# The last output pair's products in another order, and one product of the first set in column halves

## The chip, the cores and the metric

The kernel runs on one core of a Trainium2 chip. The metric is the device time of one execution in microseconds (us), median of several runs. "The span" is the time from the first to the last instruction of the one execution that the profiler recorded; it is about 1.8 us shorter than the device time of the same execution.

## The reference, cut to what matters

```python
def reference(x, w1, w2):            # x 16x256x512, w1 512x4096, w2 2048x512, all float32
    h = x @ w1
    gate, value = np.split(h, 2, axis=-1)
    h = np.maximum(gate, 0) * value
    return (h @ w2).astype(np.float32)
```

## The kernel before

Both matrix products are done block by block with seven half-size products (P1 to P7) instead of eight, in float16. The 4,096 rows of x are worked off in four sets of 1,024. In each set 16 blocks fill `g` (the hidden values), and four pairs of row tiles then turn `g` into output. A checker on the side looks whether the values suit float16; if not, a slow general way runs behind a branch at the end. For these inputs the branch is taken over the general way.

```python
# the whole program: the fast way, then a branch over the general way
with ExitStack() as fast:
    unfit = fast_way(fast, tc, x2, w1, w2, out2, flag)
with tc.If(unfit > 0, label="general"):
    with ExitStack() as general:
        general_way(general, tc, x2, w1, w2, out2)
```

```python
class Block:                                   # one product of the first stage: two 512-column matmuls
    def mm(self, name, ps, fresh):
        wn, xn = WX[name]
        for b in range(2):
            nc.tensor.matmul(ps, wop[wn][:, b, self.jb * P:(self.jb + 1) * P], self.xo[xn][:, b, :],
                             start=fresh and b == 0, stop=b == 1, skip_group_check=True)
    ...
class Pair:                                    # second stage: each product is eight 256-column matmuls
    ...
    def send(self, h, c):
        nc.sync.dma_start(out=out_v[self.s, h, self.t, :, c], in_=self.o[:, h, c])
    ...
    def P2(self):                              # ScalarE evicts X into the left half of the first output
        self.o = tmp.tile([P, 2, DO], F32, name="o", tag="tmp")
        nc.scalar.activation(self.o[:, 0, :DO // 2], self.X, COPY, scale=1 / GS)
        if self.end:
            self.send(0, slice(0, DO // 2))
    ...
    def P7(self):                              # VectorE evicts Y into the right half of the second output
        nc.vector.scalar_tensor_tensor(out=self.o[:, 1, DO // 2:], in0=self.Y, scalar=1 / GS, in1=self.pu[:, 0],
                                       op0=MULT, op1=ADD)
        if self.end:
            self.send(1, slice(DO // 2, DO))

    def P4(self):                              # P4 is added to the same Y; ScalarE evicts it: the last of all
        nc.scalar.activation(self.o[:, 1, :DO // 2], self.Y, COPY, scale=1 / GS)
        self.send(1, slice(0, DO // 2 if self.end else DO))
    ...
ORDER = ("P1 0, P1 1, P2 0, P2 1, P1 2, P5 0, P2 2, P6 0, P3 0, P7 0, P5 1, P6 1, P3 1, P7 1, P4 0, P5 2, P4 1, "
         "P6 2, P3 2, P7 2, P1 3, P4 2, P5 3, P2 3, P6 3, P3 3, P7 3, P4 3")
LAST_ORDER = ORDER.replace("P5 3, P2 3, P6 3, P3 3, P7 3", "P2 3, P6 3, P5 3, P7 3, P3 3")
```

In the last set the order thus ends: P7 2, P1 3, P4 2, P2 3, P6 3, P5 3, **P7 3, P3 3, P4 3** (product, then pair). P4 3 adds to the PSUM bank that P7 3's eviction reads, so its first matmul waits for that eviction.

## Time and profile before

| | before |
|---|---|
| time, median of 3 runs | 308.57 us (308.36 to 308.63) |
| span of the profiled run | 307.2 us |
| TensorE busy | 301.6 us, 98% |
| end of the last matmul | 303.03 us |
| last DMA packet | 305.84 us |

The profile's page of the kernel before: TensorE's busy time, the instruction-fetch queue (packets, MB, share of 16 DMA engines) and the chain of waits that ended last.

```profile
PE 301.6 (98%) x1905; PEld 184.2 (60%) x1905; DVE 236.0 (77%) x388; ACT 176.3 (57%) x348; POOL 151.2 (49%) x189
...
q8 instruction: 16, 0.26, 0.4%
...
PE 96%; DMA 2%; SPq 1%; issue 0%; ACT 0%
```

The windows of the last set and of the tail, kernel before. Columns: stretch, its length, busy us (and instructions) of each engine, granted clock, DMA share, GB/s.

```profile
232.50:303.05 70.55, 70.53 (x438) 42.42 (x436) 56.23 (x93) 32.61 (x65) 31.45 (x48) 1.00 0.14 45
303.05:307.20 4.15, 0.00 (x0) 0.00 (x0) 0.00 (x0) 0.38 (x1) 0.00 (x0) 0.94 0.23 72
```

TensorE has no hole in the last set, and it stands still for 4.15 us behind it. Those four microseconds are the tail: an eviction of 0.38 us, the last send, and the closing barrier.

The timeline of the sending queue in the tail, kernel before. Columns: start, duration of the issue, what.

```profile
299.11 1.04 SPq L370 DMA_DIRECT2D out_dram<-o  x1
...
301.84 0.33 SPq L370 DMA_DIRECT2D out_dram<-o  x1
302.65 0.33 SPq L370 DMA_DIRECT2D out_dram<-o  x1
303.48 1.34 SPq L370 DMA_DIRECT2D out_dram<-o  x1
```

These are the sends of P2, P7, P3 and P4 of the last pair. Two of the four issues are stretched from 0.33 us to over 1 us. An instruction packet of 16 KB began at 298.45 us and another at 303.15 us, shortly before each (read from the trace's packet records).

VectorE's timeline and the branch instructions, kernel before: P7's eviction, then P3's; and the closing branch in TensorE's queue (duration in ns, start).

```profile
301.39 0.42 DVE L399 SCALAR_TENSOR_TENSOR o<-Y,pu 128x256 f32<-128x256 f32 x1 [3.56 <-PE Y L362]
302.20 0.42 DVE L394 SCALAR_TENSOR_TENSOR o<-W,pu 128x256 f32<-128x256 f32 x1 [0.38 <-PE W L362]
```

```profile
L42 PEldq COMPARE_BRANCH  x1: 496/496/496, 301.9 to 301.9; - x1
```

TensorE's sequencer executed the branch at 301.89 us.

The windows of half a microsecond in the tail, kernel before (last two columns: DMA share, GB/s).

```profile
303.50:304.00 0.50, 0.00 (x0) 0.00 (x0) 0.00 (x0) 0.00 (x0) 0.00 (x0) 1.00 0.69 234
304.00:304.50 0.50, 0.00 (x0) 0.00 (x0) 0.00 (x0) 0.00 (x0) 0.00 (x0) 1.00 0.08 12
304.50:305.00 0.50, 0.00 (x0) 0.00 (x0) 0.00 (x0) 0.00 (x0) 0.00 (x0) 1.00 0.09 16
305.00:305.50 0.50, 0.00 (x0) 0.00 (x0) 0.00 (x0) 0.00 (x0) 0.00 (x0) 1.00 0.31 109
305.50:306.00 0.50, 0.00 (x0) 0.00 (x0) 0.00 (x0) 0.00 (x0) 0.00 (x0) 1.00 0.48 158
```

Most of P3's send moves before 304 us. Then only a trickle moves for 1.3 us, and the last send follows. In the packet records the trickle is 16 of the 128 packets of P3's send; of the 16 four-byte packets that follow a send's data, two came late as well (304.73 and 305.14 us, the other 14 by 303.98). That is two DMA engines' worth if a send is spread evenly over the 16 (8 packets and one four-byte packet each; an estimate from these counts, since no view names a packet's engine). Two instruction packets, of 16 KB and of 8 KB, lay before it.

### The profile page before, as it was taken

To read this page: it belongs to the slowest core of one execution; us is meant where nothing else is said; L and a number is where in the kernel's file an instruction comes from. 1 tells how busy PE (TensorE), PEld (TensorE's weight loads), DVE (VectorE), ACT (ScalarE), POOL (GpSimd) and SP (SyncE) were. 2 spreads that over 40 slices of the span, in tenths; PEclk is the share of its full clock that TensorE was granted. 3 is DMA by queue.
4 is the path that set the end of the run, shared out by engine and by line. 5 is a ranking of instruction groups with operands and counts; after the bars stand their busy time and mean duration, and the time that the engine had idled before them with its cause. 6 is when DMAs were issued, how large, how long until landed. Compare 5 with 4: busy or idle time off the path is not lost.

```text
span 307.2 us, 5283 instructions
## 1 busy us (share of the span) xinstructions
PE 301.6 (98%) x1905; PEld 184.2 (60%) x1905; DVE 236.0 (77%) x388; ACT 176.3 (57%) x348; POOL 151.2 (49%) x189
## 2 busy tenths in 40 slices
PE   8999999999999999999999999999999999999994
PEld 7744444588844444478864444458884444447883
DVE  2579888899778888887538888888536888888851
ACT  2488896455865555537855555546866555553231
POOL 2389999800068999300029889700007988700000
PEclk9999999999999999999999999999999999999999
DMA  6985779965775270001354910000325110001132
GB/s 204 358 259 179 239 171 176 229 123 80 260 209 88 69 137 3 0 0 55 136 182 108 207 34 2 0 2 9 130 101 174 35 34 0 3 1 34 54 106 87
DMA packets 35836, 32.87 MB, mean 107 GB/s; under 512 B 14432, under 2 KB 31328, under 8 KB 35680
## 3 DMA queue, kind: packets, MB, share of 16 engines
q1 hardware_dynamic: 33536, 26.22, 28.3%
q0 software_dynamic: 2272, 6.29, 11.4%
q8 instruction: 16, 0.26, 0.4%
q14 instruction: 12, 0.10, 0.1%
HBM read 27.26 MB, written 12.58 MB: 130 GB/s over the span
## 4 chain that ended last, share of the span: by engine, by line
PE 96%; DMA 2%; SPq 1%; issue 0%; ACT 0%
PE Y L250 26%; PE X L250 17%; PE W L250 17%; PE Y L362 14%; PE W L362 9%; PE X L362 9%; DMA x_A<-in_x_dram 2%; PE X L325 1%; PE W L325 1%; PE Y L325 1%; PE Y L498 0%; PE X L498 0%; SPq L217 0%; SPq L488 0%; ACT o L405 0%
## 5 line engine op out<-in xcount | busy, mean ns | idle before, releaser
L250 PEld LDWEIGHTS <-w_T 128*128 128x128 f16 x496 | 48.3, 98 | 57.3 <-POOL w_T L232 1.1
L179 POOL TENSOR_TENSOR fold<-xh 128x1024 f32<-128x1024 f16 x16 | 30.3, 1894 | 94.6 <-DMA xh<-x 93.7
L250 PE MATMUL X<-x_A,w_B 128*128 128x512 f16 x248 | 73.8, 379 | 0.0
L250 PE MATMUL Y<-x_S,w_T 128*128 128x512 f16 x220 | 65.5, 379 | 0.0
L250 PEld LDWEIGHTS <-w_B 128*128 128x128 f16 x372 | 36.3, 98 | 42.1
L277 DVE SCALAR_TENSOR_TENSOR cc<-W,pu 128x512 f32<-128x512 f32 x62 | 42.9, 691 | 21.1 <-ACT pu L271 21.1
L257 ACT COPY Y<-X 128x512 f32<-128x512 f32 x62 | 35.4, 571 | 38.2 <-PE X L250 37.9
L271 ACT ACTIVATE pu<-Y 128x512 f32<-128x512 f32 x62 | 37.1, 598 | 33.9 <-PE Y L250 33.0
L182 POOL TENSOR_TENSOR fold<-fold 128x512 f32<-128x512 f32 (+2 forms) x96 | 51.8, 539 | 7.5
L362 PEld LDWEIGHTS <-w_stage 128*128 128x128 f16 x512 | 50.0, 98 | 5.9
L287 DVE SCALAR_TENSOR_TENSOR cc<-Y,pu 128x512 f32<-128x512 f32 x62 | 42.9, 691 | 6.7
L282 DVE SCALAR_TENSOR_TENSOR g<-X,cc 128x512 f16<-128x512 f32 x62 | 42.8, 691 | 2.3
L299 DVE SCALAR_TENSOR_TENSOR g<-Y,cc 128x512 f16<-128x512 f32 x62 | 42.2, 681 | 1.8 <-PE Y L250 1.8
L362 PEld LDWEIGHTS <-g 128*128 128x128 f16 x384 | 37.5, 98 | 8.2
L264 ACT ACTIVATE pu<-W 128x512 f32<-128x512 f32 x62 | 37.2, 600 | 0.8 <-PE W L250 0.6
L250 PE MATMUL W<-x_S,w_B 128*128 128x512 f16 x124 | 36.9, 379 | 0.0
L250 PE MATMUL W<-x_S,w_T 128*128 128x512 f16 x124 | 36.9, 379 | 0.0
L250 PE MATMUL Y<-x_A,w_T 128*128 128x512 f16 x124 | 36.9, 379 | 0.0
L362 PE MATMUL X<-w,g 128*128 128x256 f16 x256 | 31.9, 273 | 0.0
L394 DVE SCALAR_TENSOR_TENSOR o<-W,pu 128x256 f32<-128x256 f32 x16 | 6.8, 423 | 19.4 <-PE W L362 19.4
L169 DVE TENSOR_TENSOR w_stage<-g 128x1024 f16<-128x1024 f16 x32 | 21.4, 684 | 0.2
L232 POOL TENSOR_TENSOR w_T<-w_stage 128x512 f16<-128x512 f32 (+1 forms) x16 | 18.7, 1173 | 2.5 <-DMA w_stage<-in_w_dram 2.5
(100 smaller groups left out, 307.5 us busy)
## 6 DMA issues: line engine op xcount, KB each, us to landing
w_stage<-in_w_dram SPq DMA_DIRECT2D x14, 512.0 KB, 6.0
out_dram<-o SPq DMA_DIRECT2D x26, 256.0 KB, 2.1
x<-in_x_dram POOLq DMA_DIRECT2D x4, 1024.0 KB, 9.1
xh<-x SPq DMA_DIRECT2D x16, 256.0 KB, 3.0
w<-in_w_dram POOLq DMA_DIRECT2D x2, 1024.0 KB, 10.2
out_dram<-o SPq DMA_DIRECT2D x12, 128.0 KB, 1.7
w_stage<-in_w_dram SPq DMA_DIRECT2D x4, 256.0 KB, 5.4
x_S<-in_x_dram SPq DMA_DIRECT2D x4, 256.0 KB, 6.5
```

What stands on the lines that cost most here:

```text
L169: eng.tensor_tensor(o[n], o[i0], o[i1], op=op)
L179: nc.gpsimd.tensor_tensor(fold, t, t, op=MULT)
L182: nc.gpsimd.tensor_tensor(fold[:, :, :m], fold[:, :, :m], fold[:, :, m:2 * m], op=ADD)
L250: nc.tensor.matmul(ps, wop[wn][:, b, self.jb * P:(self.jb + 1) * P], self.xo[xn][:, b, :], start=fresh and b == 0, stop=b == 1, skip_group ...
L257: nc.scalar.copy(out=self.Y, in_=self.X)
L264: nc.scalar.activation(self.p5, self.W, COPY, scale=GS)
L271: nc.scalar.activation(self.u2, self.Y, COPY, scale=GS)
L277: nc.vector.scalar_tensor_tensor(out=self.c12, in0=self.W, scalar=GS, in1=self.u2, op0=MULT, op1=ADD)
L282: nc.vector.scalar_tensor_tensor(out=self.g[:, self.jb, :TH], in0=self.X, scalar=0.0, in1=self.c12, op0=MAX, op1=MULT)
L287: nc.vector.scalar_tensor_tensor(out=self.c22, in0=self.Y, scalar=GS, in1=self.p5, op0=MULT, op1=ADD)
L299: nc.vector.scalar_tensor_tensor(out=self.g[:, self.jb, TH:], in0=self.Y, scalar=0.0, in1=self.c22, op0=MAX, op1=MULT)
L362: nc.tensor.matmul(ps, self.op[an][:, i], vop[wn][:, i], start=name in ("P1", "P5") and i == 0, stop=i == NJ // 2 - 1, skip_group_check=True)
```

## The change

The intent, as far as the diff shows it: P7 of the last pair, with its eviction and its send, comes four products ahead of the end in place of two, so that less is left for the last microseconds. P1 of that pair moves ahead of P7 of the pair in front to make room. In the first set each P5 is done as four matmuls of 256 columns in place of two of 512.

```diff
+        def __init__(self, xo, g, jb, in_halves=()):
...
-            for b in range(2):
-                nc.tensor.matmul(ps, wop[wn][:, b, ...], self.xo[xn][:, b, :],
-                                 start=fresh and b == 0, stop=b == 1, skip_group_check=True)
+            for c in (half, other) if name in self.in_halves else ((0, TH),):
+                for b in range(2):
+                    nc.tensor.matmul(ps[:, slice(*c)], wop[wn][:, b, ...],
+                                     self.xo[xn][:, b, slice(*c)], start=fresh and b == c[0] == 0, stop=b == 1,
+                                     skip_group_check=True)
... (the output tile is now made by whichever of P2 and P7 comes first)
-    LAST_ORDER = ORDER.replace("P5 3, P2 3, P6 3, P3 3, P7 3", "P2 3, P6 3, P5 3, P7 3, P3 3")
+    LAST_ORDER = ORDER.replace("P7 2, P1 3, P4 2, P5 3, P2 3, P6 3, P3 3, P7 3",
+                               "P1 3, P7 2, P6 3, P5 3, P7 3, P4 2, P2 3, P3 3")
...
-        blocks = {jb: Block(xo, g, jb) for jb in range(first, NJ)}
+        blocks = {jb: Block(xo, g, jb, () if s else ("P5",)) for jb in range(first, NJ)}
...
+            if s == NS - 1 and t == 3:
+                sums = (sum_of(pairs[3].op, n) for n in ("S1", "S2", "S3", "S4"))
```

The halves add 56 instructions to TensorE's program (14 blocks, two more matmuls and two more weight loads each).

More of the change, by code (lines that the diff above doesn't have):

```diff
@@ L243, in fast_way @@
     class Block:
-        def __init__(self, xo, g, jb):
-            self.xo, self.g, self.jb, self.behind = xo, g, jb, ()
+        def __init__(self, xo, g, jb, in_halves=()):
+            self.xo, self.g, self.jb, self.behind, self.in_halves = xo, g, jb, (), in_halves
         def mm(self, name, ps, fresh):
             wn, xn = WX[name]
-            for b in range(2):
-                nc.tensor.matmul(ps, wop[wn][:, b, self.jb * P:(self.jb + 1) * P], self.xo[xn][:, b, :],
-                                 start=fresh and b == 0, stop=b == 1, skip_group_check=True)
+            for c in (half, other) if name in self.in_halves else ((0, TH),):
+                for b in range(2):
+                    nc.tensor.matmul(ps[:, slice(*c)], wop[wn][:, b, self.jb * P:(self.jb + 1) * P],
+                                     self.xo[xn][:, b, slice(*c)], start=fresh and b == c[0] == 0, stop=b == 1,
+                                     skip_group_check=True)
         def P1(self):
@@ L344, in __init__ @@
         def __init__(self, s, g, t):
-            self.s, self.t = s, t
+            self.s, self.t, self.o = s, t, None
             self.end = s == NS - 1 and t != NB // 2 - 2
@@ L367, in product, with outputs @@
                     yield
+        def outputs(self):
+            if self.o is None:
+                self.o = tmp.tile([P, 2, DO], F32, name="o", tag="tmp")
         def send(self, h, c):
@@ L382, in P2 @@
         def P2(self):
-            self.o = tmp.tile([P, 2, DO], F32, name="o", tag="tmp")
+            self.outputs()
             nc.scalar.activation(self.o[:, 0, :DO // 2], self.X, COPY, scale=1 / GS)
@@ L398, in P7 @@
         def P7(self):
+            self.outputs()
             nc.vector.scalar_tensor_tensor(out=self.o[:, 1, DO // 2:], in0=self.Y, scalar=1 / GS, in1=self.pu[:, 0],
```

## The prediction

> **What bounds the kernel.** TensorE. The chain of waits is 96% TensorE, and 2% is the first load. Matmuls follow each other without a hole: in the timeline a 512-column product matmul starts every 0.216 us (0.43 us a pair) and a 256-column one every 0.109 us (0.87 us for 8), from 16.5 us to 303.05 us. The windows view shows TensorE busy 70.53 of the 70.55 us of the last set. Everything else is the head (first 16.5 us, bound by loads) and the tail: 303.05 to 307.2 us. The tail is the last eviction (ScalarE, 0.38 us), the last output DMA and the closing barrier.
>
> **The tail, closely.** The timeline of the DMA queue shows the last three sends issued at 301.84 (P7), 302.65 (P3) and 303.48 us (P4). A send's issue takes 0.33 us, but the last takes 1.34 us, and the P2 send at 299.11 took 1.04. Just before each of these two an instruction packet of 16 KB began (298.45 and 303.15 us[...]). [...] My reading: the fetch delays the earlier send's packets on one DMA engine, and the next issue waits for that. The last send's packets move at 305.3 to 305.8 us; with a 0.33 us issue they would at about 304.3 to 304.8. So up to 1.0 us lies in the tail, if the collision goes.
>
> **What the change does.**
> 1. P5 of the first set in halves: 14 blocks, each 2 matmuls of 512 columns become 4 of 256, with 28 more weight loads. 4 x 0.109 - 2 x 0.216 = 0.005 us a block, about +0.07 us in all, on the critical path (estimate from the trace's spacings; weight loads of 0.098 us stay hidden). It does not start anything earlier: P6 of block 2 still waits for POOL's T2 (0.2 us hole at 18.4 us). It adds 56 TensorE instructions, so the fetch at 298.45 should come some 28 matmuls earlier, near 295.4 us, away from the last sends.
> 2. The last pair's order. No matmul is added. P1 to P6 now has one product (0.87 us) between them; the copy needs about 0.4 us, so no hole. S3 and S4 swapped on VectorE come in time. P7's eviction and send move from 301.4 to about 299.6 and 300.1 us; the second-last pair's 256 KB send moves from 298.24 to about 300.9, and P2's send from 299.1 to 301.8. The last three sends are again 128 KB each at about 301.8, 302.65 and 303.48. P4's first matmul no longer waits for a P7 eviction that ended only 0.35 us earlier.
>
> **On the critical path.** TensorE's end: +0.07 us. The fetch at 303.15 follows TensorE's closing branch (executed at 301.89), which neither part removes; so I expect most of the last issue's stretch to stay. It may shift or vanish with the new alignment or an earlier branch: I give that 40%, worth 0.3 to 1.0 us.
>
> **Prediction.** 308.4 us, 8 in 10 between 307.5 and 308.9. Faster by over 2%: 1%; within 2%: 98%; slower: 1%.
>
> **What would show it.** Last matmul's end at 303.1 us (+0.07); no new TensorE hole after 296 us; P2's issue back to 0.33 us; the last issue 1.34 us if its fetch remains, 0.33 if not, and the span shorter by that.
>
> **What would make it wrong.** Half products costing more than 0.005 us a block; a hole before P6 or P7; the 256 KB send delaying the last ones; another fetch falling into the last 3 us.

The forecast's sum: 308.57 us for the kernel before, 0.07 more for the halves, and 0.26 less (40% of 0.65, the middle of 0.3 to 1.0) come to 308.38, the forecast's 308.4. What the trace of the kernel before shows of the queue of these 16 KB instruction packets (q8): 16 packets, 0.26 MB, each of 16 KB, the second to the 15th a mean of 252 TensorE instructions (weight loads and matmuls) apart, single steps 168 to 305. The two packets by the stretched issues took 1.34 and 1.29 us. That such a packet shares one DMA engine with a send's packets and delays them is the author's reading; no view names a packet's engine.

## The result, and the profile after

| | before | changed | ratio, 95% interval |
|---|---|---|---|
| first measurement, 6 runs each | 308.54 us (308.28 to 308.84) | 308.14 us (308.06 to 308.77) | 0.9992 (0.9979 to 1.0005) |
| again, in rounds of its own (r7), 11 and 6 runs | 308.36 us | 307.81 us | 0.9980 (0.9968 to 0.9993) |
| before against itself (r8), 11 and 6 runs | 308.36 us | 308.34 us | 0.9996 (0.9981 to 1.0011) |

A ratio is the mean time of one kernel's fast runs over that of the other's of the same rounds, so it is not quite the ratio of the medians. The change is within 2%. The first measurement's interval holds 1 and the second one's does not, so the gain is small and only just above what such rounds resolve: 0.2 us by the means of the first (308.53 to 308.29) and 0.6 us by those of the second (308.42 to 307.81).

Where the two profiled spans differ, from instruction and packet records (us):

| | to the first block matmul | to the first pair product | to the last matmul's end | to the last DMA packet | closing | span |
|---|---|---|---|---|---|---|
| before | 16.31 | 42.56 | 244.16 | 2.81 | 1.31 | 307.16 |
| changed | 16.07 | 42.62 | 244.16 | 2.14 | 1.38 | 306.37 |

The first column is no effect of the change: over the thirteen traces of the fast way it lies anywhere from 15.62 to 16.31 us. The last load on the chain of waits there took 5.41 us and was over at 8.20 us in the kernel before, 4.30 and 6.07 us in the changed one. The third column is equal to the hundredth. What differs beyond that is the second (+0.06) and the fourth (-0.67). The second scatters by itself: 42.46 to 42.57 us in the eight traces with whole products, 42.53 to 42.62 in the five with halves. The cost of the halves is therefore read from the ten blocks below and not from this column.

The changed kernel, the profile's page:

```profile
PE 300.8 (98%) x1933; PEld 186.7 (61%) x1933; DVE 235.9 (77%) x388; ACT 176.5 (58%) x348; POOL 151.4 (49%) x189
...
q8 instruction: 16, 0.26, 0.3%
...
PE 97%; DMA 1%; SPq 0%; POOL 0%; ACT 0%; issue 0%
```

The changed kernel, windows of the last set and of the tail:

```profile
232.30:302.85 70.55, 70.55 (x438) 42.50 (x436) 56.36 (x93) 32.64 (x65) 31.59 (x48) 1.00 0.14 46
302.85:306.40 3.55, 0.00 (x0) 0.00 (x0) 0.00 (x0) 0.38 (x1) 0.00 (x0) 0.83 0.24 79
```

The new order opened no hole, and the tail is 3.5 us where it was 4.15.

The changed kernel, the sending queue (P7 and P4-of-the-pair-in-front, then P2, P3, P4):

```profile
299.91 0.33 SPq L376 DMA_DIRECT2D out_dram<-o  x1
300.67 0.33 SPq L376 DMA_DIRECT2D out_dram<-o  x1
301.55 0.33 SPq L376 DMA_DIRECT2D out_dram<-o  x1
302.46 0.33 SPq L376 DMA_DIRECT2D out_dram<-o  x1
303.29 0.67 SPq L376 DMA_DIRECT2D out_dram<-o  x1
```

P2's issue is back at 0.33 us; the last is 0.67 us, half of what it was, and not 0.33.

The changed kernel, VectorE's two evictions and TensorE's closing branch:

```profile
299.46 0.42 DVE L406 SCALAR_TENSOR_TENSOR o<-Y,pu 128x256 f32<-128x256 f32 x1 [1.67 <-PE Y L364]
302.01 0.42 DVE L400 SCALAR_TENSOR_TENSOR o<-W,pu 128x256 f32<-128x256 f32 x1 [2.12 <-PE W L364]
```

```profile
L42 PEldq COMPARE_BRANCH  x1: 407/407/407, 300.7 to 300.7; - x1
```

The branch comes at 300.74 us, 2.11 us ahead of the last matmul's end in place of 1.14. The 16 KB instruction packet behind it begins 0.19 us before that end, where it had begun 0.12 us after it.

The changed kernel, windows of the tail:

```profile
303.50:304.00 0.50, 0.00 (x0) 0.00 (x0) 0.00 (x0) 0.00 (x0) 0.00 (x0) 1.00 0.45 133
304.00:304.50 0.50, 0.00 (x0) 0.00 (x0) 0.00 (x0) 0.00 (x0) 0.00 (x0) 1.00 0.13 39
304.50:305.00 0.50, 0.00 (x0) 0.00 (x0) 0.00 (x0) 0.00 (x0) 0.00 (x0) 1.00 0.75 254
305.00:305.50 0.50, 0.00 (x0) 0.00 (x0) 0.00 (x0) 0.00 (x0) 0.00 (x0) 0.69 0.00 0
```

The trickle lasts half a microsecond in place of 1.3, and nothing moves after 305 us.

The cost of the halves, groups of W's first product by shape. Kernel before:

```profile
L250 PE MATMUL W<-x_S,w_T 128*128 128x512 f16 x124 | 36.9, 379 | 0.0
```

Changed kernel:

```profile
L251 PE MATMUL W<-x_S,w_T 128*128 128x512 f16 x96 | 28.5, 379 | 0.0
L251 PE MATMUL W<-x_S,w_T 128*128 128x256 f16 x56 | 8.4, 273 | 0.0
```

28 matmuls became 56. The records of ten blocks of the first set, from the 13th block matmul into X to the one ten blocks on, take 30.216 us in every kernel with whole products and 30.267 us (30.266 in one) in every kernel with halves: 0.005 us a block.

### The profile page after: what moved, and what is told of

It reads as the page before. It is cut to its first block, busy times and chain, and to the rows that moved or that the text cites. A ratio compares the mean times of both kernels' runs of the same rounds, so it can differ in the third digit from the quotient of the medians.

```text
span 306.4 us, 5339 instructions
## 1 busy us (share of the span) xinstructions
PE 300.8 (98%) x1933; PEld 186.7 (61%) x1933; DVE 235.9 (77%) x388; ACT 176.5 (58%) x348; POOL 151.4 (49%) x189
## 4 chain that ended last, share of the span: by engine, by line
PE 97%; DMA 1%; SPq 0%; POOL 0%; ACT 0%; issue 0%
PE Y L251 26%; PE W L251 17%; PE X L251 17%; PE Y L364 14%; PE X L364 9%; PE W L364 9%; DMA w_stage<-in_w_dram 1%; PE X L327 1%; PE W L327 1%; PE Y L327 1%; PE Y L506 0%; PE X L506 0%; SPq L496 0%; PE Y L154 0%; POOL w_B L474 0%; ACT o L412 0%
## 5 line engine op out<-in xcount | busy, mean ns | idle before, releaser
L251 PEld LDWEIGHTS <-w_T 128*128 128x128 f16 x524 | 51.1, 98 | 54.6 <-POOL w_T L232 0.9
L251 PE MATMUL W<-x_S,w_T 128*128 128x512 f16 (+1 forms) x152 | 36.9, 340 | 0.0
```

The costliest lines, as they stand in the source:

```text
L251: nc.tensor.matmul(ps[:, slice(*c)], wop[wn][:, b, self.jb * P:(self.jb + 1) * P], self.xo[xn][:, b, slice(*c)], start=fresh and b == c[0] ...
```

## The experiments

Theory W: P4's wait for P7's eviction held back TensorE's sequencer, and with it the closing branch; the new order frees the branch, the fetch behind it comes earlier and is over earlier, and the last sends suffer less. Rival I: what helps is the shift of the instruction stream by 56 instructions. Rival S: what helps is how the last sends are spaced.

The table holds the tail of every trace of the fast way, in us from the last matmul's end. "Fetch" is the last 16 KB instruction packet. r-numbers are the experiments below.

| kernel | branch starts | branch took | fetch | fetch took | last issue | last DMA packet | that less the fetch's end |
|---|---|---|---|---|---|---|---|
| before | -1.14 | 0.50 | 0.12 to 1.41 | 1.29 | 1.34 | 2.81 | 1.40 |
| before again, r8 | -1.14 | 0.50 | 0.34 to 1.27 | 0.93 | 0.33 | 2.32 | 1.05 |
| halves alone, r2 | -1.15 | 0.41 | 0.22 to 1.56 | 1.34 | 0.33 | 2.62 | 1.06 |
| P7 late, r4 | -1.14 | 0.41 | 0.20 to 1.13 | 0.93 | 0.33 | 2.19 | 1.05 |
| changed | -2.11 | 0.41 | -0.19 to 0.74 | 0.93 | 0.67 | 2.14 | 1.40 |
| changed again, r7 | -2.11 | 0.41 | -0.19 to 0.74 | 0.93 | 0.67 | 2.14 | 1.40 |
| last send on ScalarE, r6 | -2.11 | 0.41 | -0.19 to 0.74 | 0.93 | 0.38 | 2.14 | 1.40 |
| order alone, r1 | -2.11 | 1.00 | -0.36 to 1.15 | 1.51 | 1.07 | 2.55 | 1.40 |
| old order without the wait, r3 | -2.04 | 0.62 | -0.69 to 0.47 | 1.16 | 0.38 | 2.34 | 1.87 |
| P2 late, r10 | -2.02 | 1.50 | 0.20 to 1.32 | 1.12 | on ScalarE | 2.35 | 1.03 |
| no branch, r5 | none | | none | | 0.33 | 1.80 | |
| short general way, r9 | -1.14 | 0.26 | none | | 0.34 | 1.80 | |
| looped general way, r11 | -1.14 | 0.26 | none | | 0.33 | 1.92 | |

### r1_order_alone

The changed kernel with whole products:

```diff
-        blocks = {jb: Block(xo, g, jb, () if s else ("P5",)) for jb in range(first, NJ)}
+        blocks = {jb: Block(xo, g, jb) for jb in range(first, NJ)}
```

> The new order of the last pair without the half products. Theory W (the closing branch of TensorE was held back in the kernel before by P4's wait for P7's eviction; the new order frees it, so the instruction fetch that follows the branch comes earlier and collides less with the last sends): as the changed kernel: branch about 2.1 us ahead of the last matmul's end, last send's issue at most 0.8 us, last data packet 2.0 to 2.3 us after the last matmul, time 0.3 to 0.8 us below the kernel before. Rival I (it is the 56 added instructions that shift the fetches): as the kernel before: branch 1.1 us ahead, last issue 1.3 us, last packet 2.7 us after the last matmul. Rival S (it is the spacing of the last sends): as the changed kernel.

Measured: 308.20 us, ratio 0.9995 (0.9982 to 1.0008). The branch came 2.11 us ahead of the end, as W and S said and against I. But it took 1.00 us and not 0.41, the fetch behind it took 1.51 us, the last issue took 1.07 us (at most 0.8 expected of W), and the last packet came at 2.55 us, outside the 2.0 to 2.3 us expected of W. The time was 0.2 us below by the means, which these rounds do not resolve.

```profile
L42 PEldq COMPARE_BRANCH  x1: 996/996/996, 300.6 to 300.6; - x1
```

```profile
303.20 1.07 SPq L376 DMA_DIRECT2D out_dram<-o  x1
```

The order alone frees the branch; without the halves something else then holds it. The table's rows r1, r3 and r10 have one thing in common: the fetch before the last one (these 16 KB packets came 252 TensorE instructions apart in the mean in the kernel before, 254 in the changed one) ended late (300.21, 299.92 and 300.65 us), and the branch ended 1.43 to 1.44 us after it in all three. In the changed kernel, with 56 instructions more, that fetch ended at 296.67 us. So the halves seem to keep the branch from being held: three traces agree, no experiment of its own shows it. That this is how they shorten the tail is not shown, and the table speaks against it. In r1 the branch ended 0.59 us later than in the changed kernel (-1.11 against -1.70 us), and yet its fetch began earlier (-0.36 against -0.19 us). r1's tail is longer because its fetch took 1.51 us and not 0.93, and what sets that stays open.

### r2_halves_alone

The changed kernel with the old order (and the old order of the sums).

```diff
+    LAST_ORDER = ORDER.replace("P5 3, P2 3, P6 3, P3 3, P7 3", "P2 3, P6 3, P5 3, P7 3, P3 3")
```

> The half products with the old order. Theory W and rival S: tail as in the kernel before (last issue 1.2 to 1.4 us, last packet 2.7 us after the last matmul), time within 0.2 us of the kernel before, the halves costing about 0.07 us. Rival I: tail as in the changed kernel (last issue about 0.7 us, last packet 2.1 us after), time 0.4 us or more below.

Measured: 308.45 us, ratio 1.0004 (0.9990 to 1.0018). The branch is at -1.15 us again and the last packet at 2.62 us, near the 2.7 us expected of W and S; rival I, which asked for 2.1 us and a faster time, falls. The last issue, though, was 0.33 us where W expected 1.2 to 1.4. So a stretched issue is no fixed mark of the old order (see r8).

### r3_old_order_no_wait

The kernel before, with P4 of the last pair summed into a bank of its own, so that it need not wait for P7's eviction. A quarter of that pair's output is wrong.

```diff
+            fresh = name == "P4" and self.s == NS - 1 and self.t == 3
+            if fresh:
+                self.Y = psx.tile([P, TH], F32, name="X", tag="X")[:, c]
...
-                ... start=name in ("P1", "P5") and i == 0,
+                ... start=(fresh or name in ("P1", "P5")) and i == 0,
```

> The kernel before, but the last pair's P4 is summed into a bank of its own, so that it does not wait for P7's eviction (one quarter of the last pair's output is wrong on purpose). Theory W: the branch comes about 2.1 us ahead of the last matmul's end in place of 1.14, its fetch earlier than 303.15 us, last issue at most 0.9 us, time 0.3 to 0.8 us below. Rivals I and S: tail as in the kernel before, last issue 1.2 to 1.4 us.

Measured: 308.02 us, ratio 0.9983 (0.9970 to 0.9996), 0.5 us below in the means.

```profile
L42 PEldq COMPARE_BRANCH  x1: 616/616/616, 300.7 to 300.7; - x1
```

With the old order and old spacing, taking away that one wait moved the branch from 1.14 to 2.04 us ahead and the fetch from 0.12 us after to 0.69 us before the last matmul's end. This shows the first half of W, and rivals I and S fall as causes of the earlier branch. The second half holds only in part. The fetch was over at 0.47 us, but it now hit the packets of P7's send, P3's issue was stretched instead (1.22 us), P4's went out half a microsecond late, and the last packet still came at 2.34 us.

```profile
302.39 1.22 SPq L373 DMA_DIRECT2D out_dram<-o  x1
```

### r4_p7_late

The changed kernel with P7 two products ahead of the end again.

```diff
-                               "P1 3, P7 2, P6 3, P5 3, P7 3, P4 2, P2 3, P3 3")
+                               "P1 3, P7 2, P6 3, P5 3, P4 2, P2 3, P7 3, P3 3")
```

> The changed kernel with the last pair's P7 put back to two products ahead of the end (P1, P7 of the pair in front, P6, P5, P4 of the pair in front, P2, P7, P3, P4). Theory W: P4 waits for a late P7 eviction again, branch about 1.1 us ahead of the last matmul's end, last issue 1.2 to 1.4 us, time as the kernel before within 0.2 us. Rival I: as the changed kernel, last issue 0.7 us. Rival S: the last three sends are again P7, P3, P4, so as the kernel before.

Measured: 308.30 us, ratio 1.0004 (0.9991 to 1.0017).

```profile
L42 PEldq COMPARE_BRANCH  x1: 407/407/407, 301.3 to 301.3; - x1
```

The branch fell back to 1.14 us ahead, as W said: P7's place decides it. The time is that of the kernel before. But the traced execution had a fetch of only 0.93 us, the last issue took 0.33 us and the last packet came at 2.19 us, nearly as early as in the changed kernel. One trace of a late-branch kernel therefore says little about its tail.

### r5_no_branch

The kernel before without the branch and the general way (right for these inputs only). The line that marks the branch as likely taken, a hint to the sequencer (BRANCH_PREFETCH_HINT at 0.82 us in TensorE's queue in the trace of the kernel before), goes with it; r9 below keeps both branch and hint.

```diff
-    with tc.If(unfit > 0, label="general"):
-        with ExitStack() as general:
-            general_way(general, tc, x2, w1, w2, out2)
```

> The kernel before without its closing branch (the general way is left out; the result stays right for these inputs). If the fetch after the branch is what stretches the tail: no instruction packet of 16 KB within the last 3 us, last send's issue 0.33 us, last data packet about 1.75 us after the last matmul in place of 2.76, time 0.5 to 1.0 us below the kernel before. If the stretch comes from the sends alone (rival S): issue and tail as in the kernel before.

Measured: 307.54 us, ratio 0.9970 (0.9958 to 0.9983), 0.9 us below in the means. DMA queues of this kernel from 302 to 304.5 us:

```profile
q1 hardware_dynamic: 432, 0.39, 46.4%
issues: line engine op xcount, KB each, median us to landing
out_dram<-o SPq DMA_DIRECT2D x2, 128.0 KB, 1.7
```

The same view of the kernel before had one instruction packet on each of two queues:

```profile
q1 hardware_dynamic: 276, 0.25, 30.6%
q8 instruction: 1, 0.02, 3.2%
q14 instruction: 1, 0.01, 1.1%
```

Without the two packets the last data packet comes 1.80 us after the last matmul, with the old order and the old spacing. So up to 1.0 us of the tail was instruction fetches, and spacing (rival S) alone is not what stretched it. Most of it belongs to the 16 KB packet: r11, which kept the 8 KB one, ended at 1.92 us.

### r6_last_send_on_act

The changed kernel with its very last send issued by ScalarE, behind the eviction that it sends.

```diff
-            self.send(1, slice(0, DO // 2 if self.end else DO))
+            self.send(1, slice(0, DO // 2 if self.end else DO), nc.scalar if self.s == NS - 1 and self.t == 3 else nc.sync)
```

> The changed kernel with its last send issued by ScalarE, right behind the eviction that it sends, in place of SyncE. If the stretched issue is the issuing queue waiting for the earlier send's packets on the fetch's DMA engine: last issue 0.33 to 0.5 us, last data packet 1.8 to 2.1 us after the last matmul, time 0.1 to 0.5 us below the changed kernel. If the stretch lies in the DMA engines themselves: last packet as before, 2.1 to 2.8 us after.

Measured: 308.06 us, ratio 0.9990 (0.9978 to 1.0002). In ScalarE's timeline the issue is short:

```profile
303.22 0.38 ACTq L376 DMA_DIRECT2D out_dram<-o  x1
```

Yet the last packet came at 2.14 us, to the hundredth as in the changed kernel. In the changed kernel the stretched issue is thus a symptom; the reading left is that some of the send's packets queue in the DMA engines behind the fetch. A 16 KB packet took 0.93 to 1.51 us in these traces; how a DMA engine shares its time between two queues was not shown. No view names a packet's DMA engine either, so that they share one is inferred from the counts (16 late packets in the kernel before) and not seen.

### r7_after_again

The changed kernel itself, no edit.

> The changed kernel once more, for a second trace and more times: branch again 2.1 us ahead of the last matmul's end. If the tail's size is set by the order alone, last data packet 2.1 us after the last matmul within 0.1, as in its first trace; if it is left to chance how the fetch meets the sends, anything from 1.8 to 2.8 us. Time 0.1 to 0.5 us below the kernel before.

Measured: 307.81 us, ratio 0.9980 (0.9968 to 0.9993). The tail repeats to the hundredth: branch -2.11, fetch -0.19 to 0.74, last issue 0.67, last packet 2.14 us. So does r6's, its issue aside. With this order and the halves the tail is the same in each of three traces.

### r8_before_again

The kernel before itself, no edit.

> The kernel before against itself, for a second trace and to see what five rounds resolve: ratio 1 within about 0.1%. Branch again 1.14 us ahead of the last matmul's end. If the last issue's 1.34 us is what this order always gives, again 1.2 to 1.4 us and a last packet 2.7 us after the last matmul; if it is chance, as in the two other kernels with the late branch, 0.33 us or anything between is as likely.

Measured: 308.34 us, ratio 0.9996 (0.9981 to 1.0011), so five rounds resolve about 0.15%. Its second trace:

```profile
303.15 0.33 SPq L370 DMA_DIRECT2D out_dram<-o  x1
```

The branch is at -1.14 us as ever, but the last issue takes 0.33 us and the last packet comes at 2.32 us, not 2.81. The 1.34 us from which the prediction started was one draw of several. With the late branch the four traces run from 2.19 to 2.81 us, mean 2.48.

### r9_short_general

The kernel before; the general way keeps its place behind the branch, but without its token loop (right for these inputs only).

```diff
-    for c in range(T // TH):
+    for c in range(0):
```

> The kernel before, branch kept, but the general way that it jumps over has its token loop taken out (right for these inputs, useless for others), so that the end of TensorE's program lies 1,700 instructions closer, a few instructions behind the branch. If the fetch comes of the jump to a far place: no 16 KB instruction packet in the last 3 us, last issue 0.33 us, last data packet 1.8 us after the last matmul, time 0.5 to 1.0 us below the kernel before, like the kernel without a branch. If any branch brings a fetch: as the kernel before, last packet 2.3 to 2.8 us after.

Measured: 307.80 us, ratio 0.9989 (0.9976 to 1.0002), so the time alone does not tell it from the kernel before; five of six runs lie at 307.62 to 308.14 us, one at 308.82. From 302 to 304.5 us this kernel moved no instruction packet either:

```profile
q1 hardware_dynamic: 431, 0.39, 46.3%
issues: line engine op xcount, KB each, median us to landing
out_dram<-o SPq DMA_DIRECT2D x2, 128.0 KB, 1.7
```

The branch is there, at -1.14 us; the fetch is not, and the last packet comes at 1.80 us as without a branch. So the fetch is not the branch's as such: of these kernels it is there in those whose program ends far behind. Here 1,664 matmuls and transposes of the general way lay between (8 turns of 208, counted in kernel.py), each with a weight load of its own (as in the fast way: 1,905 of each in the trace of the kernel before). The fetch at 298.45 us is gone as well, why is not shown, and P2's issue is back at 0.33 us.

### r10_p2_late_act

No halves; the pair in front keeps its old places, then P6, P5, P7, P2, P3, P4 of the last pair; last send from ScalarE.

```diff
-                               "P1 3, P7 2, P6 3, P5 3, P7 3, P4 2, P2 3, P3 3")
+                               "P7 2, P1 3, P4 2, P6 3, P5 3, P7 3, P2 3, P3 3")
```

> No half products; order P7 and P4 of the pair in front early as in the kernel before, then P6, P5, P7, P2, P3, P4 of the last pair (P7 three products ahead of P4's end), last send from ScalarE. The 256 KB send is out of the fetch's way and P4 waits for nothing late: branch 2.1 us ahead of the last matmul's end, fetch about 0.7 us ahead (as in the old order without the wait), ended 0.2 to 0.5 us after; last data packet 1.8 to 2.0 us after the last matmul, time 0.5 to 0.8 us below the kernel before. If the fetch is as late as in the changed kernel (0.2 us ahead): last packet 2.1 to 2.5 us after, time as the changed kernel's.

Measured: 309.01 us, ratio 1.0023 (1.0010 to 1.0036): slower, a miss. The branch started 2.02 us ahead, but it took 1.50 us, held as in r1 after an earlier fetch that ended late:

```profile
L42 PEldq COMPARE_BRANCH  x1: 1501/1501/1501, 300.6 to 300.6; - x1
```

In this trace freeing the branch brought little: the fetch behind it began at 0.20 us, as with a late branch. The traced execution was the fastest of the five (308.14 us, last packet 2.35 us), so why the other four took 308.95 to 309.36 us is not seen in any trace and stays open.

### r11_compact_general and r12_general_forced

The kernel before with its general way rewritten as two nested hardware loops: 128 rows of x a turn, inside it 128 hidden units a turn. The fast way is untouched. The general way is much slower than before but as general, and the program's end lies 70 TensorE instructions behind the branch (which no trace shows). r12 is the same with the verdict forced, to see that the loops compute what they should.

```diff
+    with tc.For_i(0, T, P) as r:
+        ... load and transpose 128 rows
+        with tc.For_i(0, H, P) as h:
+            ... load 128 columns of gate and of value, 128 rows of w2; two products, gate, third product; add to the output
+        nc.gpsimd.dma_start(out=out2[bass.ds(r, P), :], in_=o)
```

In r12 the count of fitting values is asked to be five more than there are:

```diff
-        n = P * st.shape[1]
+        n = P * st.shape[1] + 5
```

> The kernel before (old order, whole products), its general way rewritten as two nested hardware loops, so that the program's end lies 70 TensorE instructions behind the branch in place of 1,700 and the kernel still serves every input. If the far jump is the cause: no 16 KB instruction packet in the last 3 us, last issue 0.33 us, last data packet 1.8 us after the last matmul, time 0.5 to 1.0 us below the kernel before, and 0.2 to 0.5 us below what the changed kernel showed. If the loops' own branches bring a fetch as well: tail 2.1 to 2.8 us, time as before.

> The same with its verdict forced, so that the looped general way runs: correct if those loops compute what they should. It takes several milliseconds, since each of its 512 turns loads its weights again; no theory hangs on its time.

Measured: r11 308.27 us, ratio 0.9986 (0.9971 to 1.0001). There is no 16 KB packet in its tail (one begins at 308.10 us, 1.75 us after the span's end), the last issue is 0.33 us, and the last packet comes at 1.92 us; an 8 KB instruction packet of another queue (q14) fell into the tail. That is 0.4 us below by the means (308.56 to 308.18), less than the 0.5 to 1.0 expected. It does not beat the changed kernel by anything that these runs resolve (0.9992 and 0.9980), although its traced tail is shorter. r12 gave the right result in 6,374 us (state unknown, one run), so the loops work.

## Why the prediction was right or wrong

**Right: the range and the class.** 308.4 us was forecast with 307.5 to 308.9; 308.14 us came, and 307.81 us in the second measurement. The range also held the kernel before's own 308.54 us, so that it was met says little about the mechanism; the entries below do.

**Right: the cost of the halves.** 0.005 us a block and 0.07 us in all was the estimate; ten blocks took 0.051 us longer in every trace.

**Right: TensorE's order has no new hole, and the sends' places.** P7's eviction came at 299.46 us (forecast 299.6), the 256 KB send at 300.67 (300.9), P2's at 301.55 (301.8). The fetch of 298.45 us came at 295.68 us (295.4), and P2's issue went back to 0.33 us.

**Right in kind, given too little weight: an earlier branch.** The prediction saw that P4 no longer waits for a late P7 eviction and named "an earlier branch" as a way in which the last fetch could shift, but put 40% on any shift and expected "most of the last issue's stretch to stay". In the changed kernel the branch came 0.97 us earlier in relation to the last matmul, three times out of three. r3 and r4 show that P7's eviction held it.

**Half right: the stretched issue.** The step "the next issue waits for that" fits every trace. All nine stretched issues after 298 us end 0.36 to 0.38 us after the end of a 16 KB fetch: P4's in before, changed, r7 and r1, P3's in r3, P2's in before, r8, r3 and r5. The last packet then came 1.02 to 1.03 us after the end of the last issue, as in r5 without a late fetch (1.02). In the kernel before the whole last send moved so late (the windows from 305 us on), so the stretch probably did set the end there; only in the changed kernel was that tested, by r6, and there it did not.

What failed is the fork: "1.34 us if its fetch remains, 0.33 if not", and "with a 0.33 us issue they would [move] at about 304.3 to 304.8". In the changed kernel the fetch remained and the issue took 0.67 us. r2, r4 and r8 kept the fetch with a 0.33 us issue, and their last packets came at 2.19 to 2.62 us, not the 1.80 us of a tail without a fetch. What counts either way is when the fetch is over. In the table the last packet comes 1.03 to 1.06 us after the fetch's end where the last issue was short, and 1.40 us after it where it was stretched (0.38 us to the issue's end, then 1.02) and in r6; r3, whose P3 issue was hit, stands aside.

The new order ends the fetch at 0.74 us where the late-branch traces end it at 1.13 to 1.56. Against those of them with a short last issue it gives 0.35 us of that back. A reading, not tested: its fetch meets P2's send too, whose completion came at 1.93 us, where that of P7's, in about that place, had come at 0.50 to 0.67 us. P3's send is met in every trace with the fetch (completed at 2.23 to 2.75 us, against 1.32 us in r5 and r9).

**Wrong: one trace taken for the rule.** "The last takes 1.34 us" held in one of two traces of the kernel before. The likely size of the gain in the tail is the mean of its two traces, 2.57 us, less 2.14, so 0.43 us, less 0.07 for the halves. The two measurements, 0.2 and 0.6 us, lie on both sides of that 0.36.

**Right: what lies in the tail at most.** 1.0 us was named; the kernels without the fetch end 1.0 us sooner than the first trace (1.80 against 2.81).

**Open.** What sets the fetch's own duration, 0.93 us in five traces and up to 1.51 in others. What sets its start: it began 0.71 to 1.51 us after the branch's end, and latest so in the changed kernel, where the branch came 0.97 us earlier than in the kernel before but the fetch only 0.31 us (0.53 us against r8). r1 and r10 freed the branch as well, and their fetches ended at 1.15 and 1.32 us, no earlier than with a late branch; so the earlier branch is shown, and that it alone shortened the changed kernel's tail is not. How the halves help, if they do: r1's time is not told apart from the changed kernel's. Why r10's untraced runs were slow.

## What to carry to other kernels

When compute ends and only the last sends are left, look for instruction packets in the last microseconds: a fetch that a closing branch to a far place sets off cost up to 1.0 us there (last packet at 2.14 to 2.81 us, 1.80 without a fetch), and it can be moved by freeing the engine's sequencer from its last wait (it began 0.3 to 1.0 us earlier in the changed kernel and r3 than in the kernel before's two traces, and between those two in r10) or taken away by keeping the jump short (no 16 KB packet in the tail of r9 and r11). Take a second trace of the kernel before you build an argument on one stretched instruction; here the same kernel's tail differed by 0.5 us between two traces. And do not take a long issue for the whole cause: move it to another queue and see whether the end moves with it.

## What the traces show of the closing branch and its fetch

- TensorE never waited for a 16 KB fetch in the last set (busy 70.53 of 70.55 us in the kernel before, with four such packets begun there, 237.51 to 298.45 us). But the last 16 KB fetch of these traces is a DMA packet of 0.93 to 1.51 us, and the sends pay for it: where one began around the last matmul's end, the last DMA packet came at 2.14 to 2.81 us, against 1.80 us without (r5, r9).
- In the kernel before, with a branch hint, TensorE executed its next instructions at 303.07 and 303.22 us, before the fetch (303.15 to 304.44 us) was over. The far jump still set off a fetch (none when the target lay near, r9), but TensorE did not stand still for it. Whether an earlier fetch had already brought the target (the hint was executed at 0.82 us) no view tells.
- TensorE's closing branch took 257 to 262 ns with a near target (r11, r9), 407 to 501 ns with a far one, 616 to 1,501 ns when it ended 1.43 to 1.44 us after an earlier fetch (r3, r1, r10); GpSimd's took 45 ns and VectorE's 90 ns.
- With no late wait the branch ran 2.02 to 2.11 us ahead of the last matmul's end; in the changed kernel 33 weight loads and matmuls began after it. In the kernel before, where P4's first matmul, the 15th instruction before the branch, waits for VectorE, it was 1.14 us and 16. How far it can run ahead, and what limits that, was not shown.
